# A hybrid decoder block on one core: prices of the mixer's planner, a gated unit's activation in quarters, paired squares, longer rows of conditioning weights

## The chip, the core and the metric

The kernel runs on one core of one Trainium2 chip. The metric is the device time of one execution in microseconds (us). The core has five engines that each take their instructions in order: TensorE (PE; its weight loads are shown apart, as PEld), VectorE (DVE), ScalarE (ACT), GpSimd (POOL) and SyncE (SP, which here only issues DMA transfers). PE runs at one of two clock levels, 1.2 or 2.4 GHz; the profile shows the granted clock as a share of the higher one.

## The reference

One decoder layer for 512 tokens of 1024 features, in float32.

```python
mod = silu(c) @ w_ada + b_ada            # 1024 -> 6 x 1024: shift, scale, gate, twice
h = rmsnorm(x) * (1 + scale1) + shift1
P = h @ w_in                             # u (512) | q, k, v (512 each) | z (512) | 8 gate columns
y = s5(u)                                # diagonal complex state-space layer, 32 groups of 16
y = gelu(y); y = y * sigmoid(y @ w_glu + b_glu)          # the gated unit
q, k, v = silu(causal_conv4(q, k, v)); q, k = l2norm(q), l2norm(k)    # 4 heads of 128
o = gated_delta_rule(q, k, v, decay, beta)               # state 128 x 128 per head
o = rmsnorm(o) * silu(z)
x = x + gate1 * (concat[y, o] @ w_out)
h = rmsnorm(x) * (1 + scale2) + shift2
x = x + gate2 * moe(h)    # best of 4 groups, in it the best 2 of 8 experts; 32 experts of 1024-256-1024
out = rmsnorm(x)
```

The 32 experts' weights are 3 MB each and are all read.

## The kernel before

Tokens are in four tiles of 128. The work has four stages that share the engines in this order.

**Head** (up to about 90 us): the first third of the conditioning (`Ada.load`, `Ada.block`), the norm of x, and the first six of the 20 column groups of `w_in` (`Proj.head`): u, and two heads of q.

**Mixer.** A planner writes the order of the work (`Sched`, line 201). It holds a filler, a generator that issues one accurate product after another, and a list of chains, generators that issue a few instructions and then give the time (or a condition) at which they can go on. `Sched.step` takes the first chain, by `prio`, whose time has come, else one step of the filler. Time is the planner's own clock (`Clock`, line 131): `ck.pe` advances with each product by a price in cycles (`Pe.matmul`, line 178), and `ck.op` prices each operation of another engine as a start plus a rate per element (`COST`, line 134). `ck.cur` is when the chain at hand would be through. The order so written is the priority with which the framework's scheduler places the instructions in the engines' queues.

The filler (`fill` in `run_all`) issues, in this order: the other 14 column groups of `w_in` (`Proj.groups`; 24 products of 128x512 each, as three products of a high and a low part of each operand make an accurate one), and waits; then the gated unit (`Out.glu`) and the output product of the state-space half (`Out.half`). The chains are:

- the state-space layer in four quarters: `S5.builds` makes a quarter's matrices on DVE and POOL (with a check product CB<-VX on PE and a detour through DRAM, `Kd`), `S5.mains` applies them (W<-Ug, transposes of Gs, a scan on DVE, a product with `two`, transposes of Y into `yc`). Two slots hold a quarter's matrices; the second is there only after the projections.
- the delta rule (`Gdn.run`): gates, decay matrices, a triangular inverse that goes through DRAM (`Nd`, `Xd`), then a chain over the four chunks and its output product (`Out.tile`).
- the rest of the conditioning, `Ada.part(1)` and `Ada.part(2)`, at the lowest priority. Each has 16 steps; a step loads 512 KB of `w_ada` into one of two buffers (line 454) and makes four products of 32x256 side by side into four column groups of one PSUM bank, and pauses `PACE` = 2 us of the planner's clock. In a part the four column groups hold the four quarters q of 2048 output columns, 512 columns each; z is the half of these 512. A row of a load is thus four pieces of 256 floats, 1 KB each. At the end the bias is loaded by POOL's queue and added by DVE, and POOL's queue stores the result's rows (`gd`). `part(2)` must be done before the filler goes on to the gated unit.
- the conv of each head (`Proj.conv`), after its column group: a scaled copy on ACT, three multiply-adds on DVE, SiLU and, for q and k, a square on ACT. `late` (line 668) then sums the squares over the partitions, a product with a block of ones of 32 columns, and ACT copies the result to the head's 32 partitions of `ssq` or `ssk`. The staged heads of q (`Proj.staged`) do so outside the filler. The tiles `xp` and `cy` share a ring of three buffers.

SP's queue is one and in order: the loads of `w_in` (raw), of `w_ada` (ad), the detours (Kd, W, Nd, Bs, Xd, X), the weights of the gated unit and the output product (woraw), and then the experts (`Moe.dma`, line 1723). Each stands until its buffer is free. The experts' first buffers come free when the delta rule's last step is issued.

**Router** (from about 389 us): DVE finds the experts and the places of the tokens.

**Experts** (from 414 us): 16 blocks of 128 places each, in order of slots; a load of an expert waits for its slot.

In the trace's lines L183 is `Pe.matmul`, L188 `Pe.transpose`, L170 every operation of DVE, ACT and POOL in the mixer, so tiles tell them apart; L1937 is an expert's product.

Of the kernel before, what the change touches and what calls it, by code (L numbers as in the profile page):

```python
# [13 lines left out]
AF = mybir.ActivationFunctionType  # L14
# [25 lines left out]
def ap_(t, off, dims):  # L40
    return bass.AP(tensor=t.tensor, offset=t.offset + off, ap=[list(d) for d in dims])
# [89 lines left out]
class Clock:  # L131


    COST = {"vector": (0.065, 1 / 960), "scalar": (0.07, 1 / 1200), "gpsimd": (0.1, 1 / 470)}

    def __init__(self):
        self.pe = self.cur = self.cols = 0.0
        self.tick, self.warm = 0, False
        self.free = dict.fromkeys(self.COST, 0.0)

# [14 lines left out]
    def op(self, e, n):  # L155
        a, b = self.COST[e]
        self.free[e] = max(self.free[e], self.pe) + a + b * n
        self.cur = max(self.cur + a + b * n, self.free[e]) + 0.13
# [15 lines left out]
class Pe:  # L174
# [3 lines left out]
    def matmul(self, out, lhsT, rhs, **kw):  # L178
        n, m = (int(np.prod(t.shape[1:])) for t in (rhs, lhsT))
        f = 1 if rhs.dtype == F32R else 4  # L180
        part = (1 if m > 64 else 0.5 if m > 32 else 0.25) * (0.5 if lhsT.shape[0] <= 64 else 1)
        self.ck.tensor(part * max(f * n, 2 * m), f * n * lhsT.shape[0] / 128)
        return self.eng.matmul(out, lhsT, rhs, **kw)  # L183

    def transpose(self, out, x, ident):
# [206 lines left out]
class Ada:  # L392
# [48 lines left out]
    def part(self, b):  # L441
        k, nc, a = self.k, self.k.nc, self.k.a
        if b == 1:
            self.un = k.unit("ad", [128, 2, 4, 256])
            self.n = 0
        pm = k.ps.tile([128, 512], F32, name="fa", bufs=1)
        N = 2 * KC
        w = []

        def load(i):  # L450
            z, kc = divmod(i, KC)
            t = self.un[:, self.n % 2]
            self.n += 1
            nc.sync.dma_start(t, self.wv[:, kc, b * 2048:(b + 1) * 2048].rearrange("p (q c) -> p q c", q=4)[:, :, z * 256:(z + 1) * 256])
            w.append(t)
        for i in range(N):
            while len(w) < min(N, i + 2):
                load(len(w))
            z, kc = divmod(i, KC)
            for q in range(4):  # L460
                k.pe.matmul(pm[32 * q:32 * q + 32, z * 256:(z + 1) * 256], self.csb[:, kc], w[i][:, q], start=(kc == 0), stop=(kc == KC - 1))
            t = k.ck.pe + PACE
            yield lambda: k.ck.pe >= t
        modr = self.un.rearrange("p s q c -> p (s q c)")[:, (self.n % 2) * 1024:(self.n % 2) * 1024 + 512]
        self.n += 1
        nc.gpsimd.dma_start(modr, ap_(a["b_ada"], b * 2048, [[512, 4], [0, 32], [1, 512]]))
        nc.vector.tensor_add(modr, pm, modr)

        for i, (b_, q) in enumerate(((1, 0), (2, 2), (1, 2), (2, 0))):
            if b_ == b:  # L470
                nc.gpsimd.dma_start(self.gd[i], modr[32 * q:32 * q + 64:32, :])
        if b == 2:
            k.drop("ad")
            self.done = True
# [7 lines left out]
class Proj:  # L482


    def __init__(self, k, stg, A):
        self.k, self.stg, self.A = k, stg, A
        nc, a = k.nc, k.a
        self.wv = a["w_in"][0].rearrange("(k p) n -> p k n", p=128)
        cwr = stg.tile([48, 128], F32, name="cwr")
        nc.scalar.dma_start(cwr, a["conv_w"][0].rearrange("w (j p) -> (w j) p", p=128))  # L490
        pcw = k.ps.tile([128, 512], F32, name="b")
        k.pe.transpose(pcw[:, 0:48], cwr, k.ident[:48, :48])
        self.cw = stg.tile([128, 12, 4], F32, name="cw")
        nc.vector.tensor_copy(self.cw, pcw[:, 0:48].rearrange("p (w j) -> p j w", j=12))
        self.n = self.m = self.lates = 0
        self.done, self.gated, self.closed = dict(qT=0, kT=0, vT=0, zT=0), False, False
        self.whl = [k.unit(f"whl{i}", [128, 2, 1024], F32R) for i in range(2)]
        hh = [k.unit(f"h{i}", [128, 4, T], F32R) for i in range(4)]
        self.hhi = [hh[i // 4][:, i % 4, :] for i in range(8)]
        self.hlo = [hh[2 + i // 4][:, i % 4, :] for i in range(8)]  # L500
        self.out, self.between = {}, []

    def close(self):
        self.k.drop("h0", "h1", "h2", "h3", "whl0", "whl1", "raw2")
# [148 lines left out]
    def conv(self, xp, j0, name, sdst, h):  # L653

        k, nc, stg = self.k, self.k.nc, self.stg
        dst = self.dst(name)
        y = stg.tile([128, T], F32, name="cy", tag="c2", bufs=NC2)
        cw = self.cw[:, j0 + h, :]
        nc.scalar.activation(y, xp[:, 0:T], AF.Copy, scale=cw[:, 0:1])
        for w in range(1, 4):  # L660
            nc.vector.scalar_tensor_tensor(y, xp[:, w:w + T], cw[:, w:w + 1], y, op0=ALU.mult, op1=ALU.add)
        nc.scalar.activation(dst[:, h, :], y, AF.Silu)
        if sdst is None:
            self.done[name] += 1
            return None
        nc.scalar.activation(y, dst[:, h, :], AF.Square)

        def late():
            pss = k.ps.tile([128, 512], F32, name="b")
            k.pe.matmul(pss[0:32, :], k.ones[:, 0:32], y, start=True, stop=True)  # L670
            nc.scalar.copy(sdst[32 * h:32 * h + 32, :], pss[0:32, :])
            self.done[name] += 1
        return late

    def staged(self, what, xps):
        for (c0, *x), xp in zip(what, xps):
            late = self.conv(xp, *x)
            yield 0.0
            late()
            yield 0.0  # L680
        self.k.drop("xp")

    def qkv(self, c0, j0, name, sdst, h):
# [812 lines left out]
class Out:  # L1496
# [71 lines left out]
    def glu(self, yc):  # L1568
        k, nc = self.k, self.k.nc
        v = nc.vector  # L1570
        nc.scalar.activation(yc, yc, AF.Gelu_apprx_tanh)
        hi = self.hi
        self.lo = lo = k.unit("y5lo", [128, 4, T], F32R)
        for q in range(4):
            p = k.ps.tile([128, 512], F32, name="fb", bufs=2)
            for kq in range(4):
                k.pe.matmul(p, self.wg[:, kq, q * 128:(q + 1) * 128], yc[:, kq, :], start=(kq == 0), stop=(kq == 3))
                yield
            th = self.op.tile([128, 512], F32, name="mx", bufs=2)
            nc.scalar.activation(th, p, AF.Tanh, scale=0.5, bias=self.bgc[:, q:q + 1])  # L1580
            v.scalar_tensor_tensor(th, th, 1.0, yc[:, q, :], op0=ALU.add, op1=ALU.mult)
            nc.scalar.activation(hi[:, q, :], th, AF.Copy, scale=0.5)
            v.scalar_tensor_tensor(lo[:, q, :], th, 0.5, hi[:, q, :].bitcast(F32), op0=ALU.mult, op1=ALU.subtract)
        k.drop("wg", "yc")
        self.feed()

    def add(self, t, w, nh, yh, yl, sq=None):

# [664 lines left out]
```

## Time and profile before

| | us |
|---|---|
| median of the runs | 690.23 |
| lowest | 689.15 |
| the profiled execution | 692.85 |
| its span, first to last instruction | 691.0 |

| engine | busy us | share of the span |
|---|---|---|
| PE | 573.2 | 83% |
| DVE | 351.3 | 51% |
| POOL | 190.9 | 28% |
| ACT | 184.3 | 27% |

The first queue of the hardware's DMA moved 159.14 MB. The shares are averages over the stages, which have different limits; what a change of the mixer is worth is read from the mixer's own stretch and from what waits for its end.

### The profile page before, as it was taken

How to read it: one execution, taken by the hardware profiler on the slowest of the kernel's cores; microseconds unless marked ns; L12 is line 12 of the kernel's file. 1: busy time of each engine (PE TensorE's matmuls, PEld its weight loads, DVE VectorE, ACT ScalarE, POOL GpSimd, SP SyncE). 2: the span in 40 equal slices, each digit the busy share in tenths (PEclk: the TensorE clock that was granted, in tenths of full speed). 3: DMA queues.
4: the chain of work that ended last, by engine and by line, in shares of the span. 5: the costliest groups of instructions: out<-in, count | busy, mean ns of one | idle time of the engine just before them, and what ended most of it. 6: DMA issues, size and time to landing. Idle time of an engine off the chain costs nothing. (4 is left out here: it accounts for less than half of the span.)

```text
span 691.0 us, 10248 instructions
## 1 busy us (share of the span) xinstructions
PE 573.2 (83%) x3825; PEld 327.1 (47%) x3825; DVE 351.3 (51%) x853; ACT 184.3 (27%) x348; POOL 190.9 (28%) x238
## 2 busy tenths in 40 slices
PE   2998998999999679979989619999999998555720
PEld 1666564566766458865867613333333332111100
DVE  3255965377879275765763483333334464111036
ACT  5333444445533024254334300000000000010031
POOL 5000692424536210030685320111111111000004
PEclk9999999999999969989999858999999999768775
DMA  9995236765597613110139997699999999999785
GB/s 287 233 285 160 62 91 197 215 182 161 171 274 196 154 58 131 32 43 22 48 130 415 419 422 284 240 406 396 339 415 418 409 382 403 395 402 413 287 307 206
DMA packets 97491, 174.25 MB, mean 252 GB/s; under 512 B 17236, under 2 KB 75224, under 8 KB 85152
## 3 DMA queue, kind: packets, MB, share of 16 engines
q1 hardware_dynamic: 90096, 159.14, 64.9%
q0 software_dynamic: 6496, 11.78, 5.0%
q10 hardware_dynamic: 848, 2.66, 1.0%
q8 instruction: 31, 0.51, 0.3%
q14 instruction: 20, 0.16, 0.1%
HBM read 166.62 MB, written 15.32 MB: 263 GB/s over the span
## 5 line engine op out<-in xcount | busy, mean ns | idle before, releaser
L1937 PE MATMUL pu<-gw,xb 128*32 128x512 f32 (+1 forms) x800 | 133.9, 622 | 18.6 <-DMA gw<-in_w_up 17.8
L183 PE MATMUL fb<-h,whl 128*128 128x512 f32 x336 | 92.2, 417 | 0.0
L183 PEld LDWEIGHTS fb<-h,whl 128*128 128x128 f32 x336 | 62.4, 194 | 28.2 <-issue 16.7
L1937 PE MATMUL py<-dw,hT 128*32 128x512 f32 (+1 forms) x400 | 64.7, 625 | 10.6 <-DMA dw<-in_w_down 9.6
L1937 PEld LDWEIGHTS pu<-gw,xb 128*32 128x32 f32 (+1 forms) x800 | 31.4, 119 | 81.5 <-issue 68.8
L1957 DVE TENSOR_TENSOR xb<-py,G2p 128x512 f32<-128x512 f32 x32 | 22.1, 691 | 66.2 <-PE py L1940 66.1
L1946 POOL DMA_INDIRECT Yrows<-yb,goal x16 | 16.5, 1031 | 141.3 <-DVE yb L2002 111.4
L2002 DVE TENSOR_TENSOR yb<-py,gt2r 128x512 f32<-128x512 f32 x32 | 22.1, 692 | 51.2 <-PE py L1937 51.2
L1943 POOL DMA_INDIRECT xr<-Xrows,tok x16 | 17.2, 1072 | 98.2 <-PE py L1940 85.1
L1982 ACT ACTIVATE sg<-pu 128x256 f32<-128x256 f32 x16 | 6.1, 383 | 140.8 <-PE pu L1937 140.8
L1937 PEld LDWEIGHTS py<-dw,hT 128*32 128x32 f32 (+1 forms) x400 | 17.3, 121 | 54.6 <-issue 35.5
L183 PE MATMUL pj<-h,whl 128*128 128x512 f32 x144 | 40.0, 431 | 0.5 <-ACT h L170 0.3
L170 DVE SCALAR_TENSOR_TENSOR cy<-xp,cw,cy 128x512 f32<-128x512 f32 x36 | 30.7, 858 | 7.7 <-ACT cy L170 7.2
L183 PEld LDWEIGHTS pj<-h,whl 128*128 128x128 f32 x144 | 28.7, 206 | 10.8 <-issue 1.6
L1991 ACT COPY hT<-ph 128x256 f32<-128x256 f32 x16 | 6.0, 372 | 101.7 <-PE ph L1940 101.7
L1940 PEld LDWEIGHTS py<-ident,xr 128*128 128x128 f32 x128 | 17.2, 196 | 25.6 <-issue 14.9
L183 PE MATMUL fa<-ad,cs 128*32 128x256 f32 x256 | 21.7, 398 | 6.8 <-DMA ad<-in_w_ada 6.8
L170 POOL TENSOR_TENSOR wol<-woraw,woh 128x512 fp32r<-128x512 f32 x16 | 21.6, 1367 | 10.1 <-ACT woh L170 10.1
L170 POOL TENSOR_TENSOR whl<-raw,whl 128x1024 fp32r<-128x1024 f32 x7 | 17.5, 2502 | 22.7 <-ACT whl L170 18.5
L1940 PE MATMUL py<-ident,xr 128*128 128x128 f32 x128 | 23.3, 308 | 0.0
L170 POOL TENSOR_TENSOR x<-x,mx 128x512 f32<-128x512 f32 x12 | 16.3, 1364 | 23.3 <-DVE mx L170 23.3
L1958 DVE TENSOR_TENSOR xb<-xb,sh2p 128x512 f32<-128x512 f32 x32 | 22.2, 692 | 1.1
(511 smaller groups left out, 1023.7 us busy)
## 6 DMA issues: line engine op xcount, KB each, us to landing
gw<-in_w_gate SPq DMA_DIRECT2D x32, 1024.0 KB
gw<-in_w_up SPq DMA_DIRECT2D x32, 1024.0 KB
dw<-in_w_down SPq DMA_DIRECT2D x32, 1024.0 KB
ad<-in_w_ada SPq DMA_DIRECT2D x32, 512.0 KB
raw<-in_w_ada SPq DMA_DIRECT2D x16, 512.0 KB
raw<-in_w_in SPq DMA_DIRECT2D x14, 512.0 KB
yf<-Yrows SPq DMA_DIRECT2D x8, 512.0 KB
wrow<-in_w_in SPq DMA_DIRECT2D x8, 384.0 KB
```

Source lines behind the costliest of these rows:

```text
L170: return f(*x, **y)
L183: return self.eng.matmul(out, lhsT, rhs, **kw)
L1937: pin(nc.tensor.matmul(*x, **y))
L1940: pin(nc.tensor.transpose(*x))
L1943: nc.gpsimd.indirect_dma_start(xrs[p % 2], None, Xd, bass.IndirectOffsetOnAxis(ap=tok[:, p:p + 1], axis=0), bounds_check=T - 1, oob_is_err ...
L1946: nc.gpsimd.indirect_dma_start(out, bass.IndirectOffsetOnAxis(ap=at, axis=0), y, None, bounds_check=out.shape[0] - 1, oob_is_err=False)
L1957: v.tensor_tensor(o, p, g, op=ALU.mult)
L1958: v.tensor_tensor(o, o, b, op=ALU.add)
L1982: nc.scalar.activation(sg, pu[:, 0], AF.Silu)
L1991: nc.scalar.copy(hT, ph)
L2002: v.tensor_mul(yb[:, h], py, gt2r[:, hs])
```

## The change

It does four things.

1. Prices of the planner's clock. The starts of DVE, ACT and POOL go from 0.065, 0.07 and 0.1 us to 0.2, 0.2 and 0.3 us, DVE's rate from 1/960 to 1/1000 us per element; products are priced 1.1 times (those of the accurate form) or 1.05 times their columns.
2. Squares. The first head of a pair leaves its square in `self.mates`; the second's `late` makes both products, into neighbouring column groups of one bank, and one copy of 64 partitions.
3. Conditioning. z is now the half of 2048 columns, and the four quarters q are 256 neighbouring columns each, so a load's rows are 1024 floats, 4 KB. The bias comes in four loads on SP's queue in place of one on POOL's; the stores pick the rows accordingly.
4. Gated unit. The activation of `yc` is made in four quarters, and the planner's clock waits before a quarter's first use, and again behind the unit.

```diff
-    COST = {"vector": (0.065, 1 / 960), "scalar": (0.07, 1 / 1200), "gpsimd": (0.1, 1 / 470)}
+    COST = {"vector": (0.2, 1 / 1000), "scalar": (0.2, 1 / 1200), "gpsimd": (0.3, 1 / 470)}
...
-        self.ck.tensor(part * max(f * n, 2 * m), f * n * lhsT.shape[0] / 128)
+        self.ck.tensor(part * max((1.1 if f == 1 else 1.05) * f * n, 2 * m), f * n * lhsT.shape[0] / 128)
...
-            nc.sync.dma_start(t, self.wv[:, kc, b * 2048:(b + 1) * 2048].rearrange("p (q c) -> p q c", q=4)[:, :, z * 256:(z + 1) * 256])
+            nc.sync.dma_start(t, self.wv[:, kc, b * 2048 + z * 1024:b * 2048 + (z + 1) * 1024].rearrange("p (q c) -> p q c", q=4))
...
-        nc.gpsimd.dma_start(modr, ap_(a["b_ada"], b * 2048, [[512, 4], [0, 32], [1, 512]]))
+        for q in range(4):
+            nc.sync.dma_start(modr[32 * q:32 * q + 32].rearrange("p (z c) -> p z c", z=2), ap_(a["b_ada"], b * 2048 + q * 256, [[0, 32], [1024, 2], [1, 256]]))
         nc.vector.tensor_add(modr, pm, modr)
-        for i, (b_, q) in enumerate(((1, 0), (2, 2), (1, 2), (2, 0))):
+        for i, (b_, z) in enumerate(((1, 0), (2, 1), (1, 1), (2, 0))):
             if b_ == b:
-                nc.gpsimd.dma_start(self.gd[i], modr[32 * q:32 * q + 64:32, :])
+                nc.gpsimd.dma_start(self.gd[i].rearrange("x (q c) -> (x q) c", c=256), modr[0:128:32, z * 256:(z + 1) * 256])
...
         nc.scalar.activation(y, dst[:, h, :], AF.Square)
+        mate = self.mates.pop((name, h ^ 1), None)
+        if mate is None:
+            self.mates[name, h] = y
+            return None
         def late():
             pss = k.ps.tile([128, 512], F32, name="b")
-            k.pe.matmul(pss[0:32, :], k.ones[:, 0:32], y, start=True, stop=True)
-            nc.scalar.copy(sdst[32 * h:32 * h + 32, :], pss[0:32, :])
-            self.done[name] += 1
+            for i, x in sorted(((h, y), (h ^ 1, mate))):
+                i = 32 * i
+                k.pe.matmul(pss[i:i + 32, :], k.ones[:, 0:32], x, start=True, stop=True)
+            i = 64 * (h // 2)
+            nc.scalar.copy(sdst[i:i + 64, :], pss[i:i + 64, :])
+            self.done[name] += 2
         return late
     def staged(self, what, xps):
         for (c0, *x), xp in zip(what, xps):
             late = self.conv(xp, *x)
-            yield 0.0
-            late()
-            yield 0.0
+            yield 1.0
+        late()
+        yield 0.0
...
-        nc.scalar.activation(yc, yc, AF.Gelu_apprx_tanh)
+        t = []
+        k.ck.free["scalar"] = max(k.ck.free["scalar"], k.ck.pe) + 1.28
+        for q in range(4):
+            nc.scalar.activation(yc[:, q], yc[:, q], AF.Gelu_apprx_tanh)
+            t.append(k.ck.free["scalar"] + 0.15)
...
             for kq in range(4):
+                while k.ck.pe < t[kq]:
+                    k.ck.pe += 0.1
+                    yield
...
         self.feed()
+        t = k.ck.free["vector"] + 0.15
+        while k.ck.pe < t:
+            k.ck.pe += 0.1
+            yield
```

## Rows read from the trace of the kernel before

**Rows 1.** Stage, length, busy us of PE, PEld, DVE, ACT, POOL, clock, DMA share, GB/s
```profile
90.00:245.50 155.50, 145.34 (x932) 95.07 (x931) 99.54 (x221) 60.36 (x105) 69.95 (x92) 0.95 0.65 182
245.50:302.00 56.50, 48.41 (x631) 40.90 (x629) 38.64 (x109) 21.04 (x51) 6.97 (x11) 0.91 0.19 68
302.00:389.50 87.50, 83.95 (x429) 67.08 (x427) 48.94 (x76) 36.18 (x76) 45.51 (x47) 0.96 0.45 175
389.50:414.20 24.70, 5.00 (x52) 4.11 (x51) 19.37 (x88) 2.79 (x4) 3.80 (x6) 0.55 1.02 421
414.20:485.20 71.00, 70.97 (x492) 23.43 (x494) 25.52 (x39) 3.78 (x10) 10.91 (x11) 0.96 0.84 326
485.20:657.00 171.80, 142.70 (x838) 44.91 (x838) 54.32 (x114) 11.33 (x26) 18.56 (x18) 0.90 0.97 389
```

**Rows 2.** Waits of SP's queue, 350 to 691 us: total us, times, longest
```profile
SPq L1723 <- PE pu L1937: 32.3, 8, 7.6
```

**Rows 3.** Waits of PE, 90 to 245.5 us
```profile
PE fa L183 <- DMA ad<-in_w_ada: 6.8, 4, 4.0
PE b L183 <- ACT cy L170: 1.8, 1, 1.8
```

**Rows 4.** Busy time in two stretches at the lower clock, columns of rows 1
```profile
238.50:245.30 6.80, 5.92 (x22) 4.15 (x23) 2.78 (x7) 0.00 (x0) 1.15 (x2) 0.51 0.08 23
252.10:258.90 6.80, 4.89 (x36) 3.74 (x36) 4.55 (x14) 2.38 (x4) 0.00 (x0) 0.51 0.26 99
```

**Rows 5.** Timeline of PE, first and last check product: start us, us, instructions
```profile
129.10 1.97 PE L183 MATMUL b<-CB,VX 128*128 128x32 f32 x16
...
270.32 1.75 PE L183 MATMUL b<-CB,VX 128*128 128x32 f32 x14
```

**Rows 6.** Timeline of PE around one head's squares
```profile
118.11 4.86 PE L183 MATMUL fb<-h,whl 128*128 128x512 f32 x20
122.90 1.05 PE L183 MATMUL b<-cy,ones 128*32 128x512 f32 x2
123.87 1.20 PE L183 MATMUL fb<-h,whl 128*128 128x512 f32 x4
125.01 0.64 PE L183 MATMUL fa<-ad,cs 128*32 128x256 f32 x8
125.58 0.74 PE L183 MATMUL fb<-h,whl 128*128 128x512 f32 x2
```

**Rows 7.** Groups of instructions: busy us, mean ns, idle before and its releaser
```profile
L170 ACT COPY ssq<-b 32x512 f32<-32x512 f32 x4 | 2.3, 574 | 3.2 <-PE b L183 3.2
```

**Rows 8.** Stretches of conditioning loads and of expert loads, columns of rows 1
```profile
100.20:104.20 4.00, 4.00 (x21) 2.98 (x24) 1.78 (x4) 1.05 (x1) 3.63 (x6) 1.00 0.92 306
...
362.00:380.00 18.00, 17.15 (x80) 14.03 (x79) 6.70 (x9) 7.21 (x16) 10.12 (x13) 1.00 1.01 417
```

**Rows 9.** Timeline of SP's queue before the late block
```profile
227.87 0.93 SPq L1210 DMA_DIRECT2D X<-Xd  x2
228.90 0.46 SPq L1003 DMA_DIRECT2D W<-Kd  x1
229.46 2.80 SPq L454 DMA_DIRECT2D ad<-in_w_ada  x1
232.31 3.63 SPq L1210 DMA_DIRECT2D X<-Xd  x2
```

**Rows 10.** Waits of POOL for the conditioning's end, 85 to 245 us
```profile
POOL gd L170 <- DVE ad L170: 11.4, 2, 10.8
```

**Rows 11.** Timeline of ACT and of PE around the gated unit
```profile
305.96 1.91 ACT L170 ACTIVATE yc<-yc 128x2048 f32<-128x2048 f32 x1
...
307.93 1.12 PE L183 MATMUL fb<-yc,wg 128*128 128x512 f32 x2 [0.26 <-ACT yc L170]
```

**Rows 12.** Timeline of DVE and of PE around one quarter's Gs
```profile
195.70 0.42 DVE L170 COPY Gs<-b 128x256 f32<-128x256 f32 x1
...
199.76 0.38 PE L188 MATMUL b<-ident,Gs 128*128 128x128 f32 x2
```

More of the change, by code (lines that the diff above doesn't have):

```diff
@@ L500, in __init__ @@
         self.hlo = [hh[2 + i // 4][:, i % 4, :] for i in range(8)]
-        self.out, self.between = {}, []
+        self.out, self.between, self.mates = {}, [], {}
     def close(self):
```

## Prediction

> **What bounds the kernel now.** I read the busy time by stage first [rows 1]. Up to 389.5 us the mixer runs; from 389.5 to 414.2 us the router, where PE has only 5 us of work and waits for a chain of DVE steps; from 414.2 us the experts. In the experts' first 71 us PE is busy all the time, and the weight transfers are what waits: the SP queue's waits show 32.3 us in which a load stood until PE had finished with its slot [rows 2]. From 485.2 us on the transfers are the bound (share 0.97). So the end hangs on two things in series: the moment when PE starts on the experts, and the transfers after that. The transfers have 32.3 us in hand that they now spend waiting, so a start that comes some us earlier moves the end by the same amount, and so does a later one. I take one for one.
>
> The start on the experts hangs on the mixer. In its stretch from 90 to 245.5 us (the projections, with everything else laid between them) PE is busy 145.3 of 155.5 us; from 245.5 to 302 us (projections used up, only chains left) 48.4 of 56.5; from 302 to 389.5 us (gated unit and output product) 84.0 of 87.5 [rows 1]. So **PE's queue is the mixer's bound**, with 21.8 us of gaps in all, plus matmuls at the lower clock. The waits of the first stretch say what makes the gaps there: 6.8 us, the longest 4.0, for a block of the conditioning weights, and 1.8 us for the squares of one head [rows 3]. Behind the long one the granted clock falls to the lower level: in 238.5 to 245.3 us it is 0.51 with PE busy 5.9 of 6.8, in 252.1 to 258.9 us 0.51 with 4.9 of 6.8 [rows 4]. At the full clock that work takes half, so 3.0 and 2.4 us are given away.
>
> One chain runs through these stretches that PE's bound does not cover: the state-space layer's four quarters, each build and main in turn. Its check product CB<-VX stands at 129.1 us for the first quarter and at 270.3 us for the last [rows 5]: 47 us a quarter. The gated unit waits for its end.
>
> **Squares of two heads side by side.** Sixteen records (eight products, two passes each) become four pairs in different column groups. One product holds PE from 122.90 to 123.87 us, 0.97 us [rows 6]. What two cost side by side is not in the trace; the nearest rows are the conditioning products, four column groups of 256 columns, which hold PE from 125.01 to 125.58 us, 0.57 us [rows 6], where half of a 512-column product would be 0.485. So three neighbours add 0.085 us for 256 columns; one neighbour for 512 adds at most 0.17. Four pairs save 4 x (0.97 - 0.17 to 0) = 3.2 to 3.9 us; I take **3.6**. Above nothing this bound is safe where PE is the bound, and the projections' products stand on both sides of it [rows 6]. The four ACT copies that fall away (0.574 us each, 2.3 us [rows 7]) save nothing: ACT is busy 60 of 155 us there. The first head's square now holds a buffer of the three-deep ring until the second is done; the next user is the second head after it, whose copy comes a whole projection later, so I price that at 0, and at up to 1.8 us (the one wait of this kind) if it bites.
>
> **Conditioning in 4 KB rows.** A stretch in which almost only 1 KB rows fly moves 306 GB/s at a share of 0.92; the experts' long rows move 417 at 1.01 [rows 8]. Per full share that is 333 against 413, so 0.5 MB takes 1.57 against 1.27 us, 0.3 us less. Thirty-two of them are 10 us of transfer, in a stretch whose share is 0.65 [rows 1]: hidden. The page "DMA: Bandwidth & Descriptors" of the Trainium skill, in its section Specifications, has transfers at line rate from 512 bytes on; by that the longer rows would give nothing, and the rows here disagree by a fifth. With either the term is 0, because the long wait has another reason: the last conditioning load is issued at 229.46 us, behind two loads of X and one of W, with two more of X after it on SP [rows 9], and its first use stands in PE's queue ahead of the last projections and of the third quarter's transposes.
>
> The bias moves from two GpSimd transfers to eight on SP (four per half), some 0.4 us each on SP, behind a slot that PE must leave; SP's loads of raw weights stand behind them. 3.2 us of SP in a stretch of 155 is hidden by their two-deep buffers; its cover gone, it costs up to 3.2. POOL is freed of two issues; what held it, 11.4 us for the sum that it stores, stays as long as PE is late with that block [rows 10].
>
> **The order.** The planner's prices rise: a DVE operation on 256 elements from 0.33 to 0.46 us, a POOL one on 512 from 1.19 to 1.39, an ACT one on 512 from 0.50 to 0.63 (0.574 in a row [rows 7]), an accurate matmul of 512 columns from 0.213 to 0.235 (twenty take 4.79 us, 0.24 each [rows 6]). Steps of a chain thus come to stand later between matmuls, nearer to when their operands are ready. What this does to each wait no view of before shows. Bounds: all 21.8 us of gaps and 5.4 us of clock go (27 us gained), or as much is added as the slower rival below gives (12 us). The nearest single row is the wait for the conditioning block: its load is placed by the planner's clock, and any order in which the second half of the conditioning is over before the solve's X loads are sent removes it. The conditioning's pause is 2 planner us, which now holds 10% fewer matmuls, so its blocks come earlier among the projections. I take two thirds of the wait and its first stretch of low clock: 4.5 + 3.0 = **7.5 us**, and nothing for the other 15 us of gaps.
>
> **Gated unit by quarters.** One activation of 1.91 us ends at 307.87, and its first product starts at 307.93 us after 0.26 us of wait [rows 11]. The first quarter could be through some 1.3 us sooner, but PE waited only 0.26 us, and had other products before. I take **0.3 us**; ACT pays three more starts, which nothing waits for. The pause after it is only in the planner.
>
> **Sum:** 3.6 + 7.5 + 0.3 = 11.4 us off the profiled execution's 692.85 us gives 681.4; this execution lies 2.6 us above the median of 690.23, so **679 us** as a median. A difference within 2% (13.8 us) is about what counts as no change here.
>
> **Rivals.**
> *The order also clears the last chains* (chance 0.22). All of the conditioning wait and both low-clock stretches go (6.8 + 5.4), and half of the 8.1 us of gaps from 245.5 to 302 us, with the squares: 6.8 + 5.4 + 4 + 3.6 + 0.3 = 20 us, 670 us. For it: POOL's queue stands 10.8 us behind that one block [rows 10], and with it the last quarter's build. Against: the gaps after 245.5 us are several small ones with different causes.
> *The state-space chain sets 302 us, not PE* (0.20). Then PE time saved among the projections comes back as waits after them, and only the gated unit's 0.3 us and a little of the stall are left: 689 us. For it: the 47 us a quarter hardly change from quarter to quarter. Against: its steps wait for PE, not PE for them: the copy Gs ends at 196.1 us and its transposes stand at 199.76 us [rows 12].
> *Slower: the chain's steps are placed too late* (0.13). A quarter has some 31 DVE, 16 POOL and 11 ACT steps; by the new prices they cost 31 x 0.12 + 16 x 0.2 + 11 x 0.13 = 8.4 us more planner time, while 42 us of planner time now hold a tenth fewer matmuls, 4.4 us real. Net 4 us per quarter, three quarters among the projections: 12 us, less the squares: 8 us, 698 us; with the longer stretch of chains at the low clock up to 704. It decides if the last quarter's check product stands later than 270 us. For it: these steps already wait 3.7 us for their place [rows 12]. Against: once the projections are used up nothing stands before them.
>
> **The numbers.** The forecast has 0.45, its own range 672 to 687. The range over all takes in the first rival with its unknowns (down to 664) and most of the slower one (up to 700). Faster by over 2% (below 676.4): most of the first rival and a quarter of the forecast, 0.30. Slower by over 2%: 0.06. Within: 0.64.
>
> **What would show it.** Squares: eight records instead of sixteen standing alone, or pairs of 0.97 to 1.14 us. Conditioning: no PE wait for ad, share and GB/s of an ad-only stretch near 413 per full share, and no low clock before the projections' end. The order: PE's first expert product near 403 us, the last check product before 262 us, the first expert load earlier by about the same 11 us. The gated unit: four activations, the first product in front of the last. Wrong if PE starts on the experts 11 us earlier and the end does not follow (the transfers are the bound from the start), or if the gaps after 245.5 us grow by what the projections save.

## The result and the profile after

| | before | after |
|---|---|---|
| median of the runs, us | 689.69 | 707.48 |
| ratio to before, 95% interval | | 1.026, 1.0216 to 1.0303 |
| the profiled execution, us | 692.85 | 708.33 |
| its span | 691.0 | 706.5 |
| PE busy, us | 573.2 | 574.6 |

The runs after lie between 704.89 and 713.19 us. One of the four runs before took 1380.61 us; the ratio is of the fast runs alone. The change makes the kernel 2.6% slower; 679 us had been forecast. PE's work took as long as before (574.6 against 573.2 us), so 14.1 of the 15.5 us by which the span grew are time in which PE does nothing.

The busy time by stage, after, in the columns of [rows 1] (the stages are cut at the same events: end of the projections, last transposes of Y, router, first expert product, and the same two lengths after it; only the first cut stands late, at the gated unit's first product, since the last projection product ends at 239.8 us and PE is busy from there to 243.0):

```profile
90.00:243.00 153.00, 139.28 (x908) 92.42 (x908) 99.38 (x212) 66.89 (x107) 59.47 (x76) 0.96 0.56 168
243.00:329.00 86.00, 68.81 (x753) 58.06 (x752) 52.20 (x145) 28.35 (x78) 15.43 (x24) 0.92 0.21 63
329.00:407.00 78.00, 70.88 (x323) 55.07 (x322) 33.17 (x48) 27.76 (x52) 41.06 (x43) 0.93 0.56 224
407.00:432.30 25.30, 5.87 (x58) 4.86 (x57) 20.11 (x89) 2.50 (x4) 3.85 (x7) 0.58 0.95 379
432.30:503.30 71.00, 70.98 (x498) 23.72 (x500) 25.93 (x40) 4.17 (x11) 10.91 (x11) 0.98 0.80 311
503.30:675.00 171.70, 143.21 (x846) 44.82 (x846) 53.98 (x113) 11.46 (x27) 18.55 (x18) 0.90 0.98 391
```

The first stage is 2.5 us shorter than in [rows 1], and yet PE has more gaps in it (13.7 against 10.2 us). The second, which before held chains only and now also the gated unit's first products, is 29.5 us longer: 86.0 against 56.5 us, its gaps 17.2 against 8.1. The third is 9.5 us shorter, because more of PE's work is done ahead of it (68.8 us busy in the second stage against 48.4); its own gaps are 7.1 us against 3.6. Router and experts are as they were. From 90 us to the first expert product it is 342.3 us against 324.2.

The check products of the four quarters on PE's timeline, after (the line in which each begins):

```profile
131.03 1.97 PE L183 MATMUL b<-CB,VX 128*128 128x32 f32 x16
178.43 1.52 PE L183 MATMUL b<-CB,VX 128*128 128x32 f32 x12
...
254.86 1.75 PE L183 MATMUL b<-CB,VX 128*128 128x32 f32 x14
...
298.65 1.52 PE L183 MATMUL b<-CB,VX 128*128 128x32 f32 x12
```

Before they stood at 129.1, 175.4, 220.1 and 270.3 us [rows 5 shows the first and the last]. From the first to the second it takes 47 us (before 46), from the second to the third 76 (45), from the third to the fourth 44 (50). The fourth check product comes 28 us later, the output product of the state-space half 26 us (350.7 against 324.5), the first expert product 18 us (432.32 against 414.23).

What the third check product waited for, after: POOL's timeline, with the last write of the part of VX that it reads (the rest of the tile is scratch for the build), then DVE's, with the last step of its quarter's build, then PE's around it:

```profile
194.75 1.87 POOL L170 TENSOR_TENSOR VX<-VX 128x256 f32<-128x256 f32 x2
```

```profile
228.02 0.43 DVE L170 SCALAR_TENSOR_TENSOR two<-two,VX 128x256 f32<-128x256 f32 x1 [0.65 <-POOL two L170]
```

```profile
246.47 1.02 PE L183 MATMUL fb<-yc,wg 128*128 128x512 f32 x2
247.34 0.60 PE L188 MATMUL b<-ident,vT 128*128 128x128 f32 x4
247.87 0.22 PE L188 MATMUL b<-ident,bgp 4*128 4x4 f32 x1
251.27 3.25 PE L188 MATMUL b<-ident,X 128*128 128x128 f32 x16 [3.18 <-issue]
254.45 0.48 PE L183 MATMUL b<-Dr,ident 16*128 16x128 f32 x2
254.86 1.75 PE L183 MATMUL b<-CB,VX 128*128 128x32 f32 x14
```

Its operands are whole at 196.6 us and the build's step ahead of it ends at 228.45. It then stands 26 us in PE's queue: behind the rest of the projections, the gated unit's first products, and the transposes of the delta rule's inverse, which wait 3.18 us themselves, for something that this view does not name. Before, the same step ended at 218.87 and the check product started at 220.10. Until it and the transposes of VX behind it have run, VX is not free for the fourth quarter. The fourth check product does not start when its operands are there either: they are whole at 268.6 us after and at 229.6 before, and it then stands 30 and 41 us in the queue.

PE's waits from 90 to 243 us, after, against [rows 3]; and SP's from 380 to 415 us (us in total, times, longest):

```profile
PE fa L183 <- DMA ad<-in_w_ada: 11.6, 7, 3.5
PE b L188 <- DVE U L170: 1.3, 1, 1.3
```

```profile
SPq L1743 <- PE b L188: 25.6, 1, 25.6
```

The wait for the conditioning's blocks, which the forecast had going, grew from 6.8 to 11.6 us. SP issues the first expert load at 352.85 us, 6.5 us earlier than before, but then stands 25.6 us for buffers that the delta rule holds: the experts' loads wait for the mixer, not the other way round.

### The profile page after: what moved, and what is told of

It is laid out like the page before. It is cut to its first block, busy times and chain, and to the rows that moved or that the text cites. A ratio compares the mean times of both kernels' runs of the same rounds, so it can differ in the third digit from the quotient of the medians.

```text
span 706.5 us, 10261 instructions
## 1 busy us (share of the span) xinstructions
PE 574.6 (81%) x3825; PEld 329.7 (47%) x3825; DVE 350.3 (50%) x853; ACT 190.8 (27%) x353; POOL 184.9 (26%) x236
## 5 line engine op out<-in xcount | busy, mean ns | idle before, releaser
L1957 PE MATMUL py<-dw,hT 128*32 128x512 f32 (+1 forms) x400 | 63.2, 616 | 10.6 <-DMA dw<-in_w_down 9.6
L183 PE MATMUL pj<-h,whl 128*128 128x512 f32 x144 | 37.9, 415 | 0.1
L170 DVE SCALAR_TENSOR_TENSOR cy<-xp,cw,cy 128x512 f32<-128x512 f32 x36 | 31.6, 882 | 10.2 <-ACT cy L170 9.6
L183 PE MATMUL fa<-ad,cs 128*32 128x256 f32 x256 | 21.3, 401 | 11.6 <-DMA ad<-in_w_ada 11.6
L1960 PEld LDWEIGHTS py<-ident,xr 128*128 128x128 f32 x128 | 17.2, 196 | 24.8 <-issue 13.2
L170 DVE TENSOR_TENSOR mx<-fb,gt1r 128x512 f32<-128x512 f32 x16 | 10.7, 689 | 30.1 <-PE fb L183 30.1
L170 POOL TENSOR_TENSOR wol<-woraw,woh 128x512 fp32r<-128x512 f32 x16 | 21.5, 1355 | 15.3 <-ACT woh L170 15.0
L183 PE MATMUL fb<-yc,wg 128*128 128x512 f32 x32 | 18.3, 715 | 7.4 <-ACT mx L170 4.9
```

Source lines behind the costliest of these rows:

```text
L170: return f(*x, **y)
L1957: pin(nc.tensor.matmul(*x, **y))
L1960: pin(nc.tensor.transpose(*x))
```

## The experiments

The theories: **P** (A in the first four expectations), the new prices place the state-space chain late and that is the loss; **B**, the bias and the rows on SP's queue; **C**, the quarters of the gated unit; **D**, the prices harm by whatever else they move. Ratios are to the kernel before, run beside it, with 95% intervals. "Behind n of 336" is a product's place in PE's queue: how many of the 336 projection products stand ahead of it.

**One part alone (e1 to e4).** Each kernel is the one before with one part of the diff in the section on the change. (In most runs one line also reads `self.t[c]` where the kernel has `self.t.pop(c)`; it issues the same instructions.) e1:

```diff
-    COST = {"vector": (0.065, 1 / 960), "scalar": (0.07, 1 / 1200), "gpsimd": (0.1, 1 / 470)}
+    COST = {"vector": (0.2, 1 / 1000), "scalar": (0.2, 1 / 1200), "gpsimd": (0.3, 1 / 470)}
-        self.ck.tensor(part * max(f * n, 2 * m), f * n * lhsT.shape[0] / 128)
+        self.ck.tensor(part * max((1.1 if f == 1 else 1.05) * f * n, 2 * m), f * n * lhsT.shape[0] / 128)
```

> The kernel before with the planner's new prices and nothing else. In its PE queue the third quarter's check product stands behind all 336 products of the projections (before: behind 296 of them), as in the changed kernel. Theory A (the prices alone make the loss, by putting the third quarter behind the projections): slower by 2 to 4%, some 703 to 715 us; third check product at 245 to 260 us in place of 220, last transposes of Y near 325 in place of 301 us. Theory B (the long rows and the bias on SP's queue hold up the solve's loads): within 1% of before. Theory C (the gated unit's quarters, made early, cost ACT tables and hold PE): within 1% of before.

712.36 us, 1.0313 (1.0274 to 1.0351): all of the loss. PE's wait for ad is 4.3 us here, less than before (6.8). Third check product at 258.87 us, fourth at 298.14, first expert product at 434.35.

e2, part 3 (rows and bias):

```diff
-            nc.sync.dma_start(t, self.wv[:, kc, b * 2048:(b + 1) * 2048].rearrange("p (q c) -> p q c", q=4)[:, :, z * 256:(z + 1) * 256])
+            nc.sync.dma_start(t, self.wv[:, kc, b * 2048 + z * 1024:b * 2048 + (z + 1) * 1024].rearrange("p (q c) -> p q c", q=4))
...
-        nc.gpsimd.dma_start(modr, ap_(a["b_ada"], b * 2048, [[512, 4], [0, 32], [1, 512]]))
+        for q in range(4):
+            nc.sync.dma_start(modr[32 * q:32 * q + 32].rearrange("p (z c) -> p z c", z=2), ap_(a["b_ada"], b * 2048 + q * 256, [[0, 32], [1024, 2], [1, 256]]))
```

> The kernel before with the conditioning in 4 KB rows and its bias on SP's queue, nothing else; its PE queue has the same order as before as far as the check products, the mains and the gated unit go. Theory A: within 1% of before, the wait of PE for the conditioning weights between 0 and 7 us. Theory B: slower by 1.5 to 3%, PE's wait for the weights above 10 us. Theory C: within 1%.

686.89 us, 0.994 (0.9907 to 0.9973). The wait for ad falls from 6.8 to 3.3 us. B falls.

e3, part 2 (squares):

```diff
+        mate = self.mates.pop((name, h ^ 1), None)
...
+            for i, x in sorted(((h, y), (h ^ 1, mate))):
```

> The kernel before with the squares in pairs, nothing else. All three theories: 3 to 5 us faster (0.4 to 0.7%) if PE's queue is the bound among the projections; 0 if the state-space chain is. The eight products hold PE for 4 us in place of 8.

693.7 us, 1.0032 (1.0005 to 1.0059). The chain is earlier (fourth check product 264.3 against 270.3 us), but the output product of its half starts at 325.4 us, no earlier than before (324.5): PE then waits 3.7 us for the gated unit's activation and 6.6 for its DVE steps, where before it waited 0.3 and 3.3.

e4, part 4 (quarters of the gated unit):

```diff
-        nc.scalar.activation(yc, yc, AF.Gelu_apprx_tanh)
+        for q in range(4):
+            nc.scalar.activation(yc[:, q], yc[:, q], AF.Gelu_apprx_tanh)
```

> The kernel before with the gated unit's activation in quarters, nothing else; in PE's queue products of the gated unit now stand between the second and the third quarter's mains. Theory A: within 1% of before, with 4 to 6 more table loads on ACT. Theory B: within 1%. Theory C: slower by 1.5 to 3%, with PE waiting several us for yc.

692.54 us, 1.0018 (0.9993 to 1.0042): nothing, and C falls.

**All but the prices (e5, and e13 with more runs).** The changed kernel with e1's diff undone.

> The changed kernel with the planner's old prices; the rows, the squares by pairs and the quarters of the gated unit are kept. On TensorE's queue the check products of the second and third quarter of the state-space chain stand behind 193 and 283 of the 336 projection products (changed kernel: 225 and 336). Theory P (the new prices place the third quarter behind the last projection, and that is the whole loss): the three other parts alone, 0.994 x 1.003 x 1.002 = 0.999 of the time before, 685 to 693 us, the third check product at 258 to 270 us less the time of its earlier place, gated unit at 300 to 308 us. Rival (the parts disturb each other, so that the squares and quarters cost once they stand together): 695 us or more, with a wait of TensorE on an eviction of the projections.

680.34 us, 0.9874 (0.9792 to 0.9957): a larger gain than the product of the parts, 0.999, and than either expectation.

> The kernel of e5_without_prices once more, word for word, with more runs. Theory G (the three parts gain together, because the squares bring the chain forward and the quarters pass it on): 0.984 to 0.991, 677 to 684 us. Rival N (their sum is what rows, quarters and squares show apart, and e5 lay at the edge of the spread): 0.992 to 0.999.

681.9 us, 0.9875 (0.9844 to 0.9906). It is no spread of the runs: the three parts gain together what they don't gain apart. It is the best version found, and beats the changed kernel by 3.6% (681.9 to 707.48).

**The same prices, the chain released earlier (e6, e8).** A chain's next step may be given out while the planner's DVE and POOL are up to 3.0 us ahead of its PE; e6 on e1, e8 on the whole change:

```diff
-        return max(self.free["vector"], self.free["gpsimd"]) < self.pe + 1.5
+        return max(self.free["vector"], self.free["gpsimd"]) < self.pe + 3.0
```

> The prices alone, as in e1_prices_alone, and one number more: a chain's next step may be given out while the planner's VectorE and GpSimd are up to 3.0 us (before: 1.5) ahead of its TensorE. The prices are the same; the third check product stands behind 306 of the 336 projection products instead of behind all. Theory P (place of the third quarter): third check product on TensorE 20 to 30 us earlier than 258.9 us, the gated unit 12 to 25 us earlier than 331.2 us, time 688 to 700 us against 712.4. Rival D (the prices harm through what else they move: ScalarE's table loads, 11 instead of 5, VectorE's order): 705 to 715 us, the gated unit still at 325 us or later.

706.9 us, 1.0272 (1.0226 to 1.0319). The third check product comes 25.6 us earlier than in e1 (233.27), as expected, but the fourth only 15.3 (282.88), the output product 10 (341.9), the first expert product 5.2 (429.17). The check product came where P expected it, but the time lies in the range of D (705 to 715 us) and not of P (688 to 700): the third quarter's place is part of the loss, and not most of it. The rest of the chain is stretched too: from the second check product to the second quarter's product with `two` it takes 43.2 us, before 37.1, and the chain's end, the last transposes of Y, is at 315.7 us, 14 us later than before (301.7), as the first expert product is 15 us later. ACT's table loads, which D names, are not the rest: there are 11 in e1, 9 in e6 and 9 before.

> The whole change, with 3.0 us in place of 1.5 us in the rule by which a chain's next step is given out. The third check product stands behind 307 of 336 projection products (changed kernel: 336). Theory P: 682 to 697 us against 707.5, third check product 20 us or more earlier than 254.9 us, gated unit's first expansion product 12 to 25 us earlier than 350.7 us. Rival D (what else the prices move): 703 to 710 us.

702.75 us, 1.0197 (1.0151 to 1.0244): third check product 20.6 us earlier, output product 11.1. The same again: above what P expected, and just under D's range.

**Which price (e7, e10).** e7 has of e1's diff only COST, so TensorE's price stays.

> Of the prices only the starts and rates of VectorE, ScalarE and GpSimd; TensorE's price per column stays as before. The second check product stands behind 253, the third behind all 336 projection products. Theory P: the starts are what puts the chain late, and TensorE's dearer columns softened it: at least as slow as e1_prices_alone, 712 to 730 us, the second check product at 190 us or later, the third at 258 us or later. Rival (the loss comes from the dearer columns, which delay everything else): 688 to 698 us.

710.4 us, 1.0332 (1.0277 to 1.0387): the starts of the three engines (and DVE's rate, which is in the same line) make the loss, without any of the dearer columns. e10 has the opposite, the dearer columns at the old starts, on the kernel of e9 (below).

> As e9_rows_quarters, and of the new prices TensorE's alone (1.1 and 1.05 times the columns); the starts stay old. Check products behind 108, 187 and 275 of the 336 (e9: 103, 205, 294). Theory P (the end follows the place of the chain's quarters): the third check product 5 us or more earlier than in e9, the fourth 3 us or more, time 2 to 6 us below e9's. Rival (any new price harms by what else it moves): 5 us or more above e9's.

686.1 us, 0.996 (0.9914 to 1.0005), e9 0.9968: TensorE's price does no harm. Third check product 9.8 us earlier than in e9, fourth 2.2, first expert product 3.4; the times don't tell the two apart.

**The old prices, the chain late (e11).** Nothing of the change; in the builds of the state-space chain each of the nine conditions is replaced, so that a step is given out only when the planner holds the one ahead of it for done:

```diff
-            yield k.ck.calm
+            yield 0.0
```

> The kernel before, at the old prices, with none of the four parts; in the builds of the state-space chain each step is given out when the planner holds the step ahead of it for done, instead of as soon as VectorE and GpSimd are less than 1.5 us ahead. The chain's quarters come late on the queues: check products behind 148, 240, 336 and 336 of the 336 projection products (before: 103, 205, 296, 336). Theory P (a late chain alone makes the loss): the third check product at 250 us or later, the fourth at 295 us or later, the gated unit's first output product 20 us or more later than 324.5 us, time 703 to 725 us. Rival (the prices themselves harm by what else they move): within 1% of the time before, 683 to 697 us.

719.86 us, 1.0403 (1.0348 to 1.0457). Check products on PE's timeline, the third and fourth:

```profile
282.60 1.97 PE L183 MATMUL b<-CB,VX 128*128 128x32 f32 x16
313.84 1.49 PE L183 MATMUL b<-CB,VX 128*128 128x32 f32 x6
```

The first expert product stands at 444.47 us, 30 us late, and the time is some 30 us longer. A late chain alone makes such a loss, and a larger one, with no price touched. So D is not needed for the loss; that nothing else moved by the prices adds to it is not shown.

**What makes e5's gain (e9, e12).** e9 is rows and quarters, e12 rows and squares, both at the old prices; their edits are those of e2 with e4 and of e2 with e3.

> The kernel before with the conditioning's rows and the quarters of the gated unit, at the old prices and with the squares one by one; check products behind 103, 205 and 294 of the 336 projection products. It splits the gain of e5_without_prices (0.987). Theory Q (the quarters shorten the stretch from the last check product to the first output product of the state-space part by some 5 us, and the rows free TensorE's wait on ad): 0.985 to 0.992, 679 to 684 us, that stretch 48 to 51 us (before: 54.2). Rival S (the squares by pairs are needed): 0.993 to 0.998, 685 to 688 us, like e2_rows_alone.

689.14 us, 0.9968 (0.9932 to 1.0003).

> The kernel before with the rows and the squares by pairs, at the old prices; the gated unit in one piece. Check products behind 93, 193 and 283 of the 336, as in e5_without_prices. Theory Q (the quarters make the difference between 0.994 and 0.987): the stretch from the last check product to the first output product of the state-space part is 54 us or longer, 0.991 to 0.998, 683 to 688 us. Rival S (the squares): 0.984 to 0.990, 678 to 683 us.

689.87 us, 0.998 (0.995 to 1.001). Neither theory: each pair gains little, and all three 1.25%. The traces say why for a part. In e12 the chain is the earliest of all (fourth check product 257.1 us), but the output product starts only at 318.7; PE stands ahead of the gated unit. e12, PE's timeline:

```profile
293.44 0.63 PE L188 MATMUL b<-ident,X 128*128 128x128 f32 x4
298.56 8.09 PE L183 MATMUL fb<-yc,wg 128*128 128x512 f32 x12 [4.48 <-ACT yc L170]
...
318.69 0.80 PE L183 MATMUL fb<-woh,y5hi 128*128 128x512 f32 x1
```

With the quarters (e13), where the same transposes of X end at 300.0 us, PE's timeline:

```profile
299.84 1.88 PE L183 MATMUL fb<-yc,wg 128*128 128x512 f32 x4
303.50 7.13 PE L183 MATMUL fb<-yc,wg 128*128 128x512 f32 x16 [1.78 <-ACT mx L170]
...
311.72 0.48 PE L183 MATMUL fb<-woh,y5hi 128*128 128x512 f32 x1
```

The output product stands 7 us earlier than in e12, although the chain is 6 us later. In e9 the chain is no earlier than before (fourth check product 269.1), so the quarters have little to pass on. Up to the first expert product e13 takes 9.6 us less than e12; 4.5 us of this are gaps (40.8 against 45.3), the rest is PE's busy time (272.4 against 277.4), on which more in the last section.

**An earlier place where the chain is early already (e14).** e13 with 1.0 in place of 1.5 us in the rule of e6.

> As e13, with 1.0 us in place of 1.5 us in the rule by which a chain's next step is given out; check products behind 93, 201 and 276 of the 336 projection products (e13: 93, 193, 283). Theory P in its simple form (the end follows the third quarter's place, us for us): third check product 3 to 6 us earlier than e13's, time 2 to 5 us lower. Rival (once the chain is early, other work of TensorE sets the end): within 0.4% of e13.

690.76 us, 1.0005 (0.9975 to 1.0035): all of e13's gain is gone, which neither side expected. The third quarter was placed earlier among the projections (276, e13: 283), but its check product started 2.5 us later, and the fourth 11 us later, behind more of the inverse's products (256 records against 160). The mixer's stretch, from 90 us to the first expert product, of e13, then of e14, columns as above:

```profile
90.00:403.10 313.10, 272.38 (x2037) 200.66 (x2035) 204.24 (x493) 125.35 (x240) 124.60 (x152) 0.94 0.55 185
```

```profile
90.00:418.70 328.70, 284.81 (x2042) 210.43 (x2041) 200.50 (x493) 125.84 (x243) 125.36 (x154) 0.91 0.53 179
```

**The check product first (e15, e16).** Its operands are whole long before its place, so a quarter's check product, its detour and the transposes of VX are given out ahead of the build's second half (the matrices in `two`). `build_a` now ends ahead of the loop that makes `two`, and `build_c` holds that loop, R8 and the release of the quarter's main; e15 on the whole change, e16 on e13:

```diff
             yield from self.build_a(q)
             yield from self.build_b(q)
+            yield from self.build_c(q)
```

> The whole change, with one step moved: in each quarter the check product CB<-VX, its detour and the transposes of VX are given out before the second half of the build (the matrices in `two`), of which they use nothing. Check products behind 81, 207, 319 and 336 of the 336 projection products (changed kernel: 109, 225, 336, 336). Theory P: the third check product 10 to 20 us earlier than 254.9 us, the fourth 8 us or more earlier than 298.6 us, time 694 to 702 us against 707.5. Rival (the chain hangs on its other steps, the mains with `two`, which come no earlier): 704 us or more.

723.06 us, 1.0438 (1.0362 to 1.0513), the slowest of all. The third check product did come 17.4 us earlier (237.49), but the fourth came 7.4 us later than in the changed kernel (306.08).

> The kernel of e5_without_prices and e13 with the same step moved; check products behind 93, 193, 277 and 336 of 336 (e13: 93, 193, 283, 336). Theory P in its simple form: fourth check product 3 us or more earlier than 263.4 us, time 674 to 680 us. Rival (where the chain is early already, the order of the other products and the clock decide): 681 us or more, or a mixer with more busy time of PE than e13's 272.4 us.

709.35 us, 1.0258 (1.0187 to 1.033). Third check product 4.1 us earlier than e13's, the fourth 10 us later (273.47), the last product with `two` 309.0 us against 290.1. The fourth's operands are whole at 227.8 us there, but ahead of it on PE's timeline stand transposes that wait for a transfer of the delta rule:

```profile
265.78 1.09 PE L188 MATMUL b<-ident,X 128*128 128x128 f32 x4 [6.17 <-DMA X<-Xd]
```

So the place of one check product is no lever. In e15 the third quarter's matrices are whole at 236.3 us, and still its main starts at 281.2 us (269.4 in the changed kernel): the main did not come along. The theory that the end follows the third quarter's place, us for us, has fallen.

What does go with the loss is the end of the chain. The last transposes of Y, and then the first expert product, come later than before by 27 and 18 us in the changed kernel, 23 and 20 in e1, 22 and 18 in e7, 14 and 15 in e6, 18 and 13 in e8, 41 and 30 in e11, 42 and 36 in e15, 12 and 16 in e16. Where the chain ends earlier than before, the experts need not follow (e3: 5 us earlier, and the experts 5 us later).

## Why the prediction was wrong

**What bounds the kernel: half right.** "One for one" from PE's start on the experts to the end held: from the first expert product to the end of the span it is 276.8 us before, 274.2 after, 273.8 in e11 and 273.3 in e13. That PE's queue is the mixer's bound did not hold as it was meant. In 90 us to the first expert product PE has 41.5 us of gaps before (324.2 less 282.71), 57.5 after (342.3 less 284.84) and 63.6 in e11 (354.4 less 290.83). The stretch, before, after and in e11, columns of [rows 1]:

```profile
90.00:414.20 324.20, 282.71 (x2037) 207.17 (x2035) 206.48 (x493) 120.36 (x236) 126.24 (x154) 0.91 0.55 178
```

```profile
90.00:432.30 342.30, 284.84 (x2035) 210.42 (x2034) 204.86 (x492) 125.50 (x240) 119.80 (x148) 0.91 0.50 170
```

```profile
90.00:444.40 354.40, 290.83 (x2040) 214.99 (x2038) 200.07 (x493) 126.46 (x242) 127.04 (x155) 0.88 0.51 167
```

Of the 18.1 us by which the stretch grew, 16.0 are gaps: 9.1 in the second stage, which the forecast had down as chains with small gaps, and 3.6 each ahead of and behind it. In e11 22 of 30 us are gaps; the rest is dearer work, at a mean clock of 0.88 against 0.91.

**The order: the step that failed.** The sum gave it -7.5 us; alone it measures 1.0313, some 21 us the other way. The text said that the steps "come to stand later between matmuls, nearer to when their operands are ready", and priced that as a gain at the wait for ad. With the prices alone that wait did fall, from 6.8 to 4.3 us, and the kernel lost 21 us all the same; in the whole change it grew to 11.6 us. Nor did the blocks come earlier to the end: the last one stands behind all 336 projection products, before behind 326. What the sum lacked is that a step later between matmuls is a chain that ends later: PE takes its queue in order, so what is placed behind the projections runs after them, whenever its operands were whole. The slower rival had this mechanism, with 0.13, and its deciding point (the last check product later than 270 us) came out: 298.6, though 270.3 is where the kernel before stood already. It too was sized too small, at 4 us a quarter and 698 to 704 us: the planner's prices don't delay every quarter evenly, but let the third slip behind the last projection: from the second check product to the third it is 76 us in place of 45. Its counter-argument, that behind the projections nothing stands before the chain, was wrong: the delta rule's products and transposes stand there, with waits of their own. And the premise of the 0.20 rival, that the state-space chain sets the end of that stretch, is what e11 shows for a late chain, though not its 689 us; the row that spoke against it (a copy ready at 196.1 us, its product at 199.76, [rows 12]) showed only that each step waits its turn, which makes the chain longer and not shorter.

**Squares: the price was right, the place was not.** Four pairs at 3.2 to 3.9 us were taken. Here is one pair, and then the two products of another, PE's timeline, after:

```profile
97.72 1.05 PE L183 MATMUL b<-cy,ones 128*32 128x512 f32 x4
...
116.56 1.04 PE L183 MATMUL b<-cy,ones 128*32 128x512 f32 x2
...
120.55 1.04 PE L183 MATMUL b<-cy,ones 128*32 128x512 f32 x2
```

Where the two heads' products stand side by side, all four records take 1.05 us, as one head's two do in [rows 6]: the pair costs no more than one. But that is one pair of four. In the others 25, 42 and 24 records of PE stand between the two products, since ACT makes the second head's square 8 to 9 us after the first's, and nothing is saved. What the diff writes side by side was not side by side in the queue. So 1 us, not 3.6.

**The rows: priced at 0, worth 0.6%.** e2 gains that much, and its wait for ad halves with the same order of PE's queue, so the transfers were not hidden altogether. Whether the longer rows do it or the bias, which is in the same edit, no run takes apart. In the stretch of [rows 8] its transfers move this (e2, busy time, columns as above):

```profile
100.20:104.20 4.00, 4.00 (x18) 3.00 (x16) 1.55 (x3) 1.05 (x1) 3.64 (x5) 1.00 0.86 318
```

That is 370 GB/s per full share, between the 333 of the 1 KB rows and the 413 of the long ones. The page "DMA: Bandwidth & Descriptors" of the Trainium skill, section Specifications, has line rate from 512 bytes on; by that nothing would change, and this row does not agree. The cost of up to 3.2 us for the eight bias loads on SP does not show.

**The gated unit: a price that holds only beside the others.** 0.3 us came from PE's wait of 0.26 us [rows 11]. Alone it measures nothing. With rows and squares it is the step from 0.998 to 0.9875, of which the gaps are about half, since then the chain is early and the wait for the activation is 4.5 us. A wait read from before is what is left of it while something else is later; it is no bound of what the edit is worth once that is gone.

**What stays open.** Which of the three starts in COST does it: they were not run one by one. What holds the mains back in e15, and how e6 and e8 keep most of the loss with the third check product early: the end of the chain is late there, but no run took its links apart. In e14 more of the inverse's products stand ahead of the fourth check product, in e16 a wait for a transfer; neither was tested alone.

## What to carry to other kernels

When a planner's prices change, find the longest chain that crosses an in-order queue and ask behind which long filler each of its links will land, and then where the chain ends: here it ended 27 us later and cost 18, and an earlier place for one link alone gave little (e6) or nothing (e15). Prices nearer to the measured times (DVE on 256 elements: 0.33 us, then 0.46, measured 0.42 [rows 12]) need not give a better order, and the order must be read from the queue itself, as must "side by side". Price a wait in the company it will have: what hides it may be the thing the same change removes.

## What the hardware showed that was not expected

PE's busy time for the same 3825 records is 573.2 us before, 574.6 after and 558.3 in e13. From 90 us to the first expert product it is 282.71 us at a mean granted clock of 0.91 before, and 272.38 at 0.94 in e13. So e13's gain is of another kind than the change's loss: its gaps there are 40.7 us against 41.5 before, and almost all of its 11.1 us is the same work at the higher clock (about 1 us of it may be the squares). These are single executions, e13's the fastest of its six and the one before 3 us above its median. But the granted clock over the whole span says the same in all runs: 0.915 to 0.928 in e13's six, with a mean of 0.922; 0.906 to 0.921 in the 17 of the kernel before beside them, and 0.904 to 0.920 in e14's twelve, with means of some 0.913 in both. e14 differs from e13 by one threshold of the planner and has 284.81 us at 0.91, and 43.9 us of gaps. Twelve transposes of Y behind the fourth check product show it, e13, then e14, PE's timeline:

```profile
273.48 1.47 PE L188 MATMUL b<-ident,Y 128*128 128x128 f32 x12
```

```profile
277.51 2.82 PE L188 MATMUL b<-ident,Y 128*128 128x128 f32 x12
```

Twelve such records take nearly twice the time, 1.47 against 2.82 us: the granted clock is 1.00 in the first stretch and 0.50 in the second. Why the one order got the higher clock more often than the other no run shows. What a new order gives or takes has to be read from busy time and gaps apart.
